# A hybrid decoder trunk on one core: 512- and 256-column matmuls in turns, and one set of PSUM pools

## The chip, the core and the metric

The kernel runs on one core of a Trainium2 chip. The metric is the device time of the whole program in microseconds (us), as the median of several runs. The engines are TensorE (PE, with its weight loads shown apart as PEld), VectorE (DVE), ScalarE (ACT), GpSimd (POOL) and SyncE (SP), whose queue issues the weight transfers here.

## The reference

256 tokens of width 2048 go through two layers in float32: layer 0 has a differential attention mixer, layer 1 a Mamba-2 mixer (SSM), and each is followed by a squared-ReLU MLP with a hidden width of 8192. Every sub-layer is preceded by an RMS norm and added to the residual.

```python
def rms_norm(x, gain):
    return x * lax.rsqrt(jnp.mean(x * x, axis=-1, keepdims=True) + EPS) * gain

def sq_relu_mlp(h, w1, w2):
    return jnp.square(jax.nn.relu(h @ w1)) @ w2
...
for i in range(DEPTH):
    x = x + mixer[i % 2](rms_norm(x, mixer_norm[i]))
    x = x + sq_relu_mlp(rms_norm(x, mlp_norm[i]), w1[i], w2[i])
```

Nearly all arithmetic lies in the products with weight matrices: the attention's q, k, v and output projections, the SSM's input and output projections, and the two matrices of each MLP.

## The kernel before, in words

**Precision.** A float32 weight tile of 128x1024 is fetched into `raw` (four buffers, by SP's queue) and split into a high part, an ACT copy (L158), and a low part, what is left, a DVE subtraction (L159); both halves lie in one tile `w` (four buffers). Activations are split in the same way, so that an activation tile holds 256 columns of high and 256 columns of low parts. A product is then high weight by both parts (512 columns) plus low weight by the high part (256 columns), summed in PSUM in float32.

**`sub_block` (L161 to L173)** multiplies eight 128x128 weight tiles into one PSUM bank: first eight 512-column matmuls with the high weights (L168), then eight 256-column matmuls with the low weights (L172). It is called 354 times, which makes 2832 matmuls of each kind. `wide_pair` and `wide_one` call it for two output blocks side by side or for one: `wide_pair` goes through the first half of the inner dimension for both blocks and then through the second half for both.

**`token_block` (L208 to L226)** is the other form, in which tokens are the stationary operand: 512 columns throughout (L222 and L224), two PSUM banks that fill side by side. It serves v, the output projections and the MLP's second matrix. `residual` (L293, and L610 in the MLP of layer 0) then adds the two banks into the tile `h` on DVE. Half of each MLP's first matrix goes through `seven` (L536 to L538), which forms seven products for a 2x2 block scheme in seven PSUM banks at once, 512 columns each; its operands are sums that DVE makes (L529 to L532 for weights, L492 to L503 for activations).

**Side work.** `Side` holds two queues of Python generators. Every `side.tick()` inside `sub_block` or `token_block` lets the first generator of each queue write down its next piece. That, and a scheduler in the compiler that may move ready matmuls ahead, sets the order of instructions on the engines. In `sub_block` the ticks stand after the fourth and the eighth 512-column matmul and after the eighth 256-column one. `norm_input` (L259) is such a generator: once a 512-column block of `h` is complete, it transposes it on PE (L268, four 128x128 transposes into an `aux` bank, twice), and `x_parts` makes the next stage's activations out of it (ACT, and DVE in L250). It gives back one tick before the first four transposes.

**PSUM.** It has eight banks. In the attention and SSM stages a pool gives four to matrix products (`mm`), another three to small work (`aux`) and one to `aux1`. Each MLP closes these and opens a pool of eight `mm` banks (the function `psum_pools`), and the SSM opens the former kind again. The first tile of a new pool waits for whatever was still using that bank in the old one.

Of the kernel before, what the change touches and what calls it, by code (L numbers as in the profile page):

```python
# [12 lines left out]
F32 = mybir.dt.float32  # L13
# [7 lines left out]
P = 128  # L21
# [67 lines left out]
def trunk_kernel(ctx: ExitStack, tc: tile.TileContext, x, xt, par, rope, qk, wv, wo, w10, w10s, w20, win, wdt, wout, w11, w11s, w21, out):  # L89
# [3 lines left out]
    const = ctx.enter_context(tc.tile_pool(name="const", bufs=1))  # L93
    actp = ctx.enter_context(tc.tile_pool(name="actp", bufs=1))
    wp = ctx.enter_context(tc.tile_pool(name="wp", bufs=1))
    psum = {}

    def psum_pools(stack, one):

        psum["mm"] = stack.enter_context(tc.tile_pool(name="ps_mm", bufs=8 if one else 4, space=PSUM))  # L100
        psum["ax"] = None if one else stack.enter_context(tc.tile_pool(name="ps_ax", bufs=3, space=PSUM))

    pa = const.tile([P, NPAR], F32, name="pa")
    nc.scalar.dma_start(out=pa[:, 0:C_MLP0], in_=par[:, 0:C_MLP0])
# [9 lines left out]
    G.affine_select(out=tri, in_=ones, pattern=[[1, P]], compare_op=ALU.is_ge, fill=0.0, base=0, channel_multiplier=-1)  # L114

    def aux():
        if psum["ax"] is None:
            return psum["mm"].tile([P, 512], F32, tag="mm", name="aux")
        return psum["ax"].tile([P, 512], F32, tag="aux", bufs=3, name="aux")

    def aux1():
        return psum["ax"].tile([P, 512], F32, tag="aux1", bufs=1, name="aux1")

    def rows(dst, cols, name):

# [23 lines left out]
    def cols(j):  # L149
        return slice(NB * j, NB * (j + 1))  # L150
# [11 lines left out]
    def sub_block(w, acts, k0, acc, start, stop):  # L162

        wh, wl = w
        for k in range(8):
            while len(acts) <= k0 + k:
                side.tick()
            PE.matmul(acc, lhsT=wh[:, k * P:(k + 1) * P], rhs=acts[k0 + k], start=(start and k == 0), stop=False)  # L168
            if k % 4 == 3:
                side.tick()  # L170
        for k in range(8):
            PE.matmul(acc[:, 0, :], lhsT=wl[:, k * P:(k + 1) * P], rhs=acts[k0 + k][:, 0, :], start=False, stop=(stop and k == 7))  # L172
        side.tick()  # L173

    def load(src, n=1):

# [4 lines left out]
        return raw  # L181

    def bank():
        return psum["mm"].tile([P, 2, T], F32, tag="mm", name="pp")

    def wide_pair(src, b, acts):

# [70 lines left out]

    def norm_input(j, gain, xs):  # L259

        for i in range(2):
            if i == 0:
                yield
            ax = aux().rearrange("p (a b) -> p a b", a=2)
            for f in range(2):
                for t in range(2):
                    c = NB * j + T * i + P * f
                    PE.transpose(ax[:, f, t * P:(t + 1) * P], h[:, t, c:c + P], ident)  # L268
            xs += x_parts(ax, 2 * j + i, gain)
            yield  # L270
        norm_square(j)
# [22 lines left out]

    scope = ExitStack()
    psum_pools(scope, False)
    xs = []
    first = [bank() for _ in range(2)]  # L300
    raw = []
# [180 lines left out]
            residual(token_block(rng(wo, 4, 8), j, sum((heads[i] for i in range(4, 8)), [])), j)  # L482
            side.add(norm_input(j, C_MLP0, xs))

    scope.close()


    def sum_parts(pool, x, dst):

# [68 lines left out]
    def mlp(xs, w1, w1s, w2, pool, after):  # L558
# [22 lines left out]
        for q in range(4):  # L581
            hid = []
            p7 = None
            wait_for = 2 if q == 0 else 0
            for j in range(8 + wait_for):
                if j >= wait_for:
                    i = j - wait_for
                    while len(sas) <= i:
                        side.tick()
                    if i == 0:  # L590
                        p7 = [bank().rearrange("p a b -> p (a b)") for _ in range(7)]
                    seven(pool, w1s[q, i], sas[i], p7, i == 0, i == 7)
                    if i == 7:
                        u = seven_out(pool, p7)
                if j < 8:
                    if j % 2 == 0:
                        r = pool.tile([P, 2, T], F32, tag="relu2", bufs=1, name="relu")
                    add_sums(r[:, j % 2:j % 2 + 1], [wide_one(w1, 8 * q + j, xs)])
                    if j % 2:
                        if q == 0 and j == 1:  # L600
                            norm_mean()
                            V.reciprocal(out=r2, in_=ms)
                        V.scalar_tensor_tensor(out=r, in0=r, scalar=0.0, in1=r, op0=ALU.max, op1=ALU.mult)
                        hid += split_pair(r)
            side.add(hidden(u, hid))
            for j in range(4):
                src = rng(w2, 8 * q + 4, 8 * q + 8) + rng(w2, 8 * q, 8 * q + 4)
                pp = token_block(src, j, hid)
                for t in range(2):
                    V.scalar_tensor_tensor(out=h[:, t, cols(j)], in0=pp[t], scalar=r2[:, t:t + 1], in1=h[:, t, cols(j)],  # L610
                                           op0=ALU.mult, op1=ALU.add)
                    if q == 3:
                        after(j, t)
# [5 lines left out]
            side.add(norm_input(j, C_MIX1, xs_next))  # L619

    with tc.tile_pool(name="mlp0", bufs=1) as mp:
        with ExitStack() as scope:
            psum_pools(scope, True)
            mlp(xs, w10, w10s, w20, mp, to_mixer)
    xs = xs_next


    scope = ExitStack()
    psum_pools(scope, False)
    with tc.tile_pool(name="ssm", bufs=1) as sp:  # L630
        dram_a = tc.dram_tile([64, T], F32, name="dram_a")
        rstd = sp.tile([P, T], F32, name="rstd")
# [237 lines left out]
        out_part(3, True)  # L870
    xs = xs_next

    scope.close()
    with tc.tile_pool(name="mlp1", bufs=1) as mp:
        with ExitStack() as scope:
            psum_pools(scope, True)
            mlp(xs, w11, w11s, w21, mp, lambda j, t: nc.sync.dma_start(out=out[:, t, cols(j)], in_=h[:, t, cols(j)]))

# [95 lines left out]
```

## Time and profile before

| what | value |
|---|---|
| median of 3 runs | 2483.77 us (2481.91 to 2486.58) |
| the profiled execution's own time | 2483.01 us |
| its span in the trace | 2481.3 us |
| granted TensorE clock, mean over the span | 1.000 |
| PE busy | 2456.4 us (99%) |
| DVE busy | 1967.4 us (79%) |
| ACT busy | 1411.4 us (57%) |
| DMA, mean rate | 190 GB/s |

The span is divided into stages by what PE does: attention up to about 412 us, the first MLP to about 1105, the SSM to about 1787, the second MLP to the end. In the rows further down, a timeline row gives start and duration of a run of like instructions; matmuls are pipelined, so that durations of neighbours overlap and the difference of two starts is what they took. In brackets stands the idle time before the instruction and what ended it. `128*128 128x512` means a stationary tile of 128x128 and 512 moving columns on 128 partitions.

### The profile page before, as it was taken

The page shows a single profiled execution, that of the slowest core. Times are in us where ns is not written, and L with a number is a line of the kernel's source. Part 1 is how long each engine was busy: PE and PEld are TensorE (multiplying, and loading weights), DVE is VectorE, ACT ScalarE, POOL GpSimd, SP SyncE. Part 2 cuts the span into 40 slices and gives each one's busy share as a digit, 9 for nine tenths or more (in the row PEclk, how much of TensorE's full clock was granted, in tenths as well). Part 3 has the DMA queues.
Part 4 walks back from the last instruction along what each step waited for, and adds up shares of the span by engine and source line. Part 5 has one row for each costly group of instructions (what it writes and reads, how often), then busy time and mean ns, then how long its engine had stood idle before and what let it go on. Part 6 is the DMA issues. An engine that isn't in the chain of part 4 may idle for free.

```text
span 2481.3 us, 33043 instructions
## 1 busy us (share of the span) xinstructions
PE 2456.4 (99%) x12462; PEld 2070.8 (83%) x12462; DVE 1967.4 (79%) x2558; ACT 1411.4 (57%) x2007; POOL 1.2 (0%) x8
## 2 busy tenths in 40 slices
PE   7999999999999999999999999999999999999999
PEld 6888887888888888888888888888788888888887
DVE  6788879977968949759886887887998696795874
ACT  6666656645545536556776576675565454554553
POOL 0000000000000000000000000000000000000000
PEclk9999999999999999999999999999999999999999
DMA  7445555465565555556555556455555556556554
GB/s 253 159 159 189 169 173 186 176 230 180 198 211 193 202 178 204 170 179 203 197 189 194 172 190 207 159 189 191 192 204 201 182 194 212 190 199 197 186 185 155
DMA packets 131120, 471.21 MB, mean 190 GB/s; under 512 B 14640, under 2 KB 14832, under 8 KB 130960
## 3 DMA queue, kind: packets, MB, share of 16 engines
q1 hardware_dynamic: 127152, 458.28, 54.8%
q10 hardware_dynamic: 3808, 10.81, 1.4%
q8 instruction: 98, 1.61, 0.3%
q14 instruction: 62, 0.51, 0.1%
HBM read 466.88 MB, written 2.16 MB: 189 GB/s over the span
## 4 chain that ended last, share of the span: by engine, by line
PE 96%; DVE 2%; DMA 1%; issue 0%; ACT 0%; ACTq 0%; SPq 0%; DVEq 0%
PE pp L222 27%; PE pp L168 26%; PE pp L172 14%; PE pp L224 13%; PE pp L536 4%; PE pp L537 4%; PE pp L538 4%; DVE w L159 1%; PE aux L774 1%; PE aux L576 1%; PE aux L141 0%; PE aux L408 0%; DMA raw<-in_w11s 0%; DMA h<-in_xt 0%; PE aux L268 0%
## 5 line engine op out<-in xcount | busy, mean ns | idle before, releaser
L159 DVE TENSOR_TENSOR w<-raw,w 128x1024 fp32r<-128x1024 f32 (+1 forms) x739 | 896.3, 1220 | 344.8 <-ACT w L158 341.8
L158 ACT CAST w<-raw 128x1024 fp32r<-128x1024 f32 (+1 forms) x739 | 776.2, 1051 | 594.9 <-PE pp L222 451.6
L222 PE MATMUL pp<-w,act 128*128 128x512 f32 x3072 | 962.7, 392 | 0.0
L168 PE MATMUL pp<-act,w 128*128 128x512 f32 x2832 | 721.7, 394 | 17.2 <-DVE act L250 13.0
L222 PEld LDWEIGHTS pp<-w,act 128*128 128x128 f32 x3072 | 574.7, 188 | 118.7 <-issue 2.1
L168 PEld LDWEIGHTS pp<-act,w 128*128 128x128 f32 x2832 | 511.5, 189 | 114.8 <-ACT w L158 17.9
L224 PE MATMUL pp<-w,act 128*128 128x512 f32 x1536 | 598.5, 390 | 0.0
L172 PEld LDWEIGHTS pp<-act,w 128*128 128x128 f32 x2832 | 384.7, 190 | 28.1 <-issue 1.7
L172 PE MATMUL pp<-act,w 128*128 128x256 f32 x2832 | 398.2, 283 | 0.0
L522 ACT CAST w<-raw 128x1024 fp32r<-128x1024 f32 (+1 forms) x256 | 241.3, 946 | 196.4 <-PE pp L172 111.0
L224 PEld LDWEIGHTS pp<-w,act 128*128 128x128 f32 x1536 | 288.6, 188 | 58.0
L523 DVE TENSOR_TENSOR w<-raw,w 128x1024 fp32r<-128x1024 f32 (+1 forms) x256 | 272.2, 1087 | 41.5 <-ACT w L522 38.5
L536 PE MATMUL pp<-w,sa 128*128 128x512 f32 x256 | 99.9, 390 | 0.0
L537 PE MATMUL pp<-w,sa 128*128 128x512 f32 x256 | 99.8, 390 | 0.0
L538 PE MATMUL pp<-w,sa 128*128 128x512 f32 x256 | 99.6, 389 | 0.0
L529 DVE TENSOR_TENSOR raw<-raw 128x1024 f32<-128x1024 f32 x64 | 78.1, 1221 | 6.8 <-DMA raw<-in_w10s 3.8
L537 PE MATMUL pp<-w,act 128*128 128x512 f32 x192 | 75.2, 391 | 0.0
L536 PE MATMUL pp<-w,act 128*128 128x512 f32 x192 | 75.1, 391 | 0.0
L538 PE MATMUL pp<-w,act 128*128 128x512 f32 x192 | 74.7, 389 | 0.0
L699 DVE SCALAR_TENSOR_TENSOR cy<-u,cwb,cy 128x256 f32<-128x256 f32 x144 | 62.9, 480 | 1.4
L205 ACT COPY relu<-pp 128x256 f32<-128x256 f32 x64 | 23.9, 373 | 63.9 <-PE pp L172 63.9
L536 PEld LDWEIGHTS pp<-w,sa 128*128 128x128 f32 x256 | 48.1, 188 | 10.5
(210 smaller groups left out, 1665.1 us busy)
## 6 DMA issues: line engine op xcount, KB each, us to landing
raw<-in_w SPq DMA_DIRECT2D x384, 512.0 KB, 3.9
raw<-in_win SPq DMA_DIRECT2D x160, 512.0 KB, 3.4
raw<-in_wout SPq DMA_DIRECT2D x64, 512.0 KB, 3.4
raw<-in_qk SPq DMA_DIRECT2D x63, 512.0 KB, 3.4
raw<-in_w10s SPq DMA_DIRECT2D x32, 768.0 KB, 4.4
raw<-in_w11s SPq DMA_DIRECT2D x32, 768.0 KB, 4.4
raw<-in_wv SPq DMA_DIRECT2D x32, 512.0 KB, 4.1
raw<-in_wo SPq DMA_DIRECT2D x32, 512.0 KB, 3.8
```

The source lines that it names most:

```text
L158: S.copy(out=wh[:, s], in_=raw[:, s])
L159: V.tensor_tensor(out=wl[:, s], in0=raw[:, s], in1=wh[:, s].bitcast(F32), op=ALU.subtract)
L168: PE.matmul(acc, lhsT=wh[:, k * P:(k + 1) * P], rhs=acts[k0 + k], start=(start and k == 0), stop=False)
L172: PE.matmul(acc[:, 0, :], lhsT=wl[:, k * P:(k + 1) * P], rhs=acts[k0 + k][:, 0, :], start=False, stop=(stop and k == 7))
L222: PE.matmul(pp[t], lhsT=act[:, 0, tok], rhs=m, start=(s + i + k == 0), stop=(s == n - 1 and i + k == 2))
L224: PE.matmul(pp[t], lhsT=act[:, 1, tok], rhs=m, start=False, stop=False)
L522: S.copy(out=w[:, 0], in_=r[:, a:a + n, :])
L523: V.tensor_tensor(out=w[:, 1], in0=r[:, a:a + n, :], in1=w[:, 0].bitcast(F32), op=ALU.subtract)
L529: V.tensor_tensor(out=r[:, 3:5, :], in0=r[:, 0:2, :], in1=bc(r[:, 6, :], 2), op=ALU.subtract)
L536: PE.matmul(pp[n], lhsT=ah, rhs=wh, start=start, stop=False)
L537: PE.matmul(pp[n], lhsT=al, rhs=wh, start=False, stop=False)
L538: PE.matmul(pp[n], lhsT=ah, rhs=wl, start=False, stop=stop)
```

## The change

Four edits:

1. In `sub_block` each step k issues its 512-column matmul and its 256-column matmul one behind the other. The three ticks stand after k = 2, 5 and 7.
2. One PSUM pool serves the whole kernel: four `mm`, three `aux` and one `aux1` bank. `psum_pools` and its scopes are gone. The seven banks of `seven` are three `mm`, three `aux` and the `aux1`.
3. `norm_input` gives back three ticks before its first transposes instead of one.
4. In each MLP the first two blocks of the first matrix that go through `wide_one` one after the other go through one `wide_pair`.

The number of instructions on each engine stays the same. The diff, without the parts that only remove the scopes:

```diff
-    psum = {}
-
-    def psum_pools(stack, one):
-
-        psum["mm"] = stack.enter_context(tc.tile_pool(name="ps_mm", bufs=8 if one else 4, space=PSUM))
-        psum["ax"] = None if one else stack.enter_context(tc.tile_pool(name="ps_ax", bufs=3, space=PSUM))
+    ps = ctx.enter_context(tc.tile_pool(name="ps", bufs=4, space=PSUM))
...
     def aux():
-        if psum["ax"] is None:
-            return psum["mm"].tile([P, 512], F32, tag="mm", name="aux")
-        return psum["ax"].tile([P, 512], F32, tag="aux", bufs=3, name="aux")
+        return ps.tile([P, 512], F32, tag="aux", bufs=3, name="aux")
...
         for k in range(8):
             while len(acts) <= k0 + k:
                 side.tick()
-            PE.matmul(acc, lhsT=wh[:, k * P:(k + 1) * P], rhs=acts[k0 + k], start=(start and k == 0), stop=False)
-            if k % 4 == 3:
+            kk = slice(k * P, (k + 1) * P)
+            PE.matmul(acc, lhsT=wh[:, kk], rhs=acts[k0 + k], start=(start and k == 0), stop=False)
+            PE.matmul(acc[:, 0, :], lhsT=wl[:, kk], rhs=acts[k0 + k][:, 0, :], start=False, stop=(stop and k == 7))
+            if k in (2, 5, 7):
                 side.tick()
-        for k in range(8):
-            PE.matmul(acc[:, 0, :], lhsT=wl[:, k * P:(k + 1) * P], rhs=acts[k0 + k][:, 0, :], start=False, stop=(stop and k == 7))
-        side.tick()
...
     def bank():
-        return psum["mm"].tile([P, 2, T], F32, tag="mm", name="pp")
+        return ps.tile([P, 2, T], F32, tag="mm", bufs=4, name="pp")
...
     def norm_input(j, gain, xs):
 
+        yield from wait(3)
         for i in range(2):
-            if i == 0:
-                yield
...
                     if i == 0:
-                        p7 = [bank().rearrange("p a b -> p (a b)") for _ in range(7)]
+                        p7 = [t for _ in range(3) for t in (bank().rearrange("p a b -> p (a b)"), aux())] + [aux1()]
...
-                    add_sums(r[:, j % 2:j % 2 + 1], [wide_one(w1, 8 * q + j, xs)])
+                    if q or j > 1:
+                        add_sums(r[:, j % 2:j % 2 + 1], [wide_one(w1, 8 * q + j, xs)])
+                    elif j == 0:
+                        add_sums(r, wide_pair(w1, 0, xs))
```

In the new file the lines move: L168 and L172 become L162 and L163, L222 and L224 become L214 and L216, L268 becomes L259, L141 becomes L134.

Three places show the order that results, all on PE. A row gives line, result, operands and shape; x2 or x4 are repetitions. First the end of the attention's output projection, where a block of `h` (`h_77`, or `h_80` after) is transposed while the next block (`pp_3517` and `pp_3518`, or `pp_3514` and `pp_3515`) is multiplied. Before:

```order
L222 MATMUL pp_3517<-w_3521,act_2371 128x512
L224 MATMUL pp_3517<-w_3521,act_2371 128x512
L222 MATMUL pp_3518<-w_3521,act_2371 128x512
L224 MATMUL pp_3518<-w_3521,act_2371 128x512
L268 MATMUL aux_3532<-ident_68,h_77 128x128 x4
L222 MATMUL pp_3517<-w_3521,act_2371 128x512
L222 MATMUL pp_3518<-w_3521,act_2371 128x512
...
L268 MATMUL aux_3546<-ident_68,h_77 128x128 x4
```

After:

```order
L214 MATMUL pp_3514<-w_3518,act_2368 128x512
L214 MATMUL pp_3515<-w_3518,act_2368 128x512
...
L214 MATMUL pp_3515<-w_3535,act_2705 128x512
L216 MATMUL pp_3515<-w_3535,act_2705 128x512
L259 MATMUL aux_3542<-ident_71,h_80 128x128 x4
L214 MATMUL pp_3514<-w_3535,act_2705 128x512
L216 MATMUL pp_3514<-w_3535,act_2705 128x512
...
L259 MATMUL aux_3556<-ident_71,h_80 128x128 x4
```

Between the block's first matmul and the first four transposes stood 8 matmuls of 512 columns, now 16.

Second, the opening of the first MLP: the last matmul of the output projection, and the first block of the MLP's first matrix. Before:

```order
L222 MATMUL pp_3614<-w_3692,act_3344 128x512
L168 MATMUL pp_3720<-act_3441,w_3725 128x512 x2
...
L168 MATMUL pp_3720<-act_3551,w_3725 128x512 x2
L268 MATMUL aux_3740<-ident_68,h_77 128x128 x4
L172 MATMUL pp_3720<-act_3441,w_3725 128x256 x2
...
L268 MATMUL aux_3762<-ident_68,h_77 128x128 x4
L168 MATMUL pp_3720<-act_3633,w_3775 128x512 x2
```

After:

```order
L214 MATMUL pp_3611<-w_3689,act_3341 128x512
L162 MATMUL pp_3712<-act_3451,w_3718 128x512
L163 MATMUL pp_3712<-act_3451,w_3718 128x256
...
L162 MATMUL pp_3713<-act_3451,w_3748 128x512
...
L163 MATMUL pp_3713<-act_3465,w_3748 128x256
L259 MATMUL aux_3757<-ident_71,h_80 128x128 x4
L162 MATMUL pp_3713<-act_3465,w_3748 128x512
...
L259 MATMUL aux_3777<-ident_71,h_80 128x128 x4
```

The last transposes stood behind eight matmuls of the first block; now a whole sub-block of the first (`pp_3712`) and three pairs of the second block (`pp_3713`) stand ahead of them.

Third, a place in the attention, the start of a sub-block of a new pair of heads. Before:

```order
L168 MATMUL pp_956<-act_180,w_1012 128x512 x2
...
L168 MATMUL pp_957<-act_180,w_1041 128x512 x2
L168 MATMUL pp_957<-act_188,w_1041 128x512
L172 MATMUL pp_956<-act_180,w_1012 128x256
L141 MATMUL aux1_1005<-sqr_975,ones_r_73 128x512
```

After:

```order
L162 MATMUL pp_953<-act_177,w_1009 128x512
L162 MATMUL pp_954<-act_177,w_1038 128x512
L214 MATMUL pp_1062<-w_1066,act_117 128x512
L216 MATMUL pp_1062<-w_1066,act_117 128x512
L397 MATMUL aux_1077<-qkn_577 128x128
...
L134 MATMUL aux1_1002<-sqr_976,ones_r_76 128x512
L163 MATMUL pp_953<-act_177,w_1009 128x256
L162 MATMUL pp_953<-act_177,w_1009 128x512
```

The first 256-column matmul of `w_1012` stood behind eleven 512-column ones; that of `w_1009` stands behind two of them and some matmuls of other work (`pp_1062` and `pp_1063` of a `token_block`, `aux_1077` of the attention scores).

## Rows read from the trace of the kernel before

**Rows 1.** The profile's page: busy time of each engine with its share of the span and instructions, and the line that divides the chain of work that ended last by engine.

```profile
PE 2456.4 (99%) x12462; PEld 2070.8 (83%) x12462; DVE 1967.4 (79%) x2558; ACT 1411.4 (57%) x2007; POOL 1.2 (0%) x8
...
PE 96%; DVE 2%; DMA 1%; issue 0%; ACT 0%; ACTq 0%; SPq 0%; DVEq 0%
```

**Rows 2.** PE's waits, grouped by what ended them: engine, result, line; waited for: us in total, times, longest us.

```profile
PE aux L268 <- DVE h L293: 3.3, 3, 1.9
PE pp L168 <- DVE h L293: 2.8, 2, 1.6
PE pp L168 <- DVE h L610: 1.4, 1, 1.4
```

**Rows 3.** The page's costliest groups: the 256-column matmuls of `sub_block`; count, busy us, mean ns of one, idle before.

```profile
L172 PE MATMUL pp<-act,w 128*128 128x256 f32 x2832 | 398.2, 283 | 0.0
```

**Rows 4.** PE's timeline from 1007 us, where a `sub_block` follows 512-column matmuls and a second one follows the first: start, duration, instruction, count.

```profile
1007.78 1.98 PE L168 MATMUL pp<-act,w 128*128 128x512 f32 x8
1009.59 1.12 PE L172 MATMUL pp<-act,w 128*128 128x256 f32 x8
1010.54 2.00 PE L168 MATMUL pp<-act,w 128*128 128x512 f32 x8
1012.38 1.11 PE L172 MATMUL pp<-act,w 128*128 128x256 f32 x8
1013.34 0.40 PE L222 MATMUL pp<-w,act 128*128 128x512 f32 x1
```

**Rows 5.** PE's timeline at two lone 256-column matmuls (L141) within 512-column ones, in the attention.

```profile
134.76 0.40 PE L141 MATMUL aux<-sor,ones_r 128*128 128x256 f32 x2
135.00 0.39 PE L222 MATMUL pp<-w,act 128*128 128x512 f32 x1
...
135.68 0.39 PE L224 MATMUL pp<-w,act 128*128 128x512 f32 x1
```

**Rows 6.** The same in the SSM.

```profile
1322.93 0.40 PE L141 MATMUL aux<-ysr,ones_r 128*128 128x256 f32 x2
1323.17 0.39 PE L222 MATMUL pp<-w,act 128*128 128x512 f32 x1
...
1324.09 1.30 PE L222 MATMUL pp<-w,act 128*128 128x512 f32 x5
```

**Rows 7.** PE's timeline in the first MLP, a lone 512-column matmul within 256-column ones.

```profile
422.48 0.40 PE L168 MATMUL pp<-act,w 128*128 128x512 f32 x1
422.71 1.46 PE L172 MATMUL pp<-act,w 128*128 128x256 f32 x11
424.01 0.63 PE L168 MATMUL pp<-act,w 128*128 128x512 f32 x2
```

**Rows 8.** PE's timeline in the first MLP: sixteen transposes in a row and the matmul behind them.

```profile
506.60 1.91 PE L576 MATMUL aux<-ident,u 128*128 128x128 f32 x16
508.26 0.48 PE L222 MATMUL pp<-w,act 128*128 128x512 f32 x1
```

**Rows 9.** The three openings of a stage with new PSUM pools on PE's timeline, at 412, 1105 and 1787 us, and DVE's timeline at the first.

```profile
411.92 1.07 PE L222 MATMUL pp<-w,act 128*128 128x512 f32 x4
414.57 2.09 PE L168 MATMUL pp<-act,w 128*128 128x512 f32 x8 [1.58 <-DVE h L293]
...
413.14 1.28 DVE L293 TENSOR_TENSOR h<-pp,h 128x512 f32<-128x512 f32 x2
...
1104.13 1.07 PE L222 MATMUL pp<-w,act 128*128 128x512 f32 x4
1106.57 2.08 PE L168 MATMUL pp<-act,w 128*128 128x512 f32 x8 [1.37 <-DVE h L610]
...
1786.73 1.07 PE L222 MATMUL pp<-w,act 128*128 128x512 f32 x4
1789.04 1.16 PE L168 MATMUL pp<-act,w 128*128 128x512 f32 x4 [1.25 <-DVE h L293]
```

**Rows 10.** PE's timeline at the second norm transposes of the attention, and DVE's there.

```profile
388.04 0.39 PE L224 MATMUL pp<-w,act 128*128 128x512 f32 x1
390.35 0.33 PE L268 MATMUL aux<-ident,h 128*128 128x128 f32 x1 [1.93 <-DVE h L293]
390.95 0.55 PE L268 MATMUL aux<-ident,h 128*128 128x128 f32 x3 [0.27 <-DVE h L293]
...
381.90 1.23 DVE L529 TENSOR_TENSOR raw<-raw 128x1024 f32<-128x1024 f32 x1 [2.94 <-DMA raw<-in_w10s]
...
389.61 1.28 DVE L293 TENSOR_TENSOR h<-pp,h 128x512 f32<-128x512 f32 x2
```

**Rows 11.** The same place in the SSM: PE, then DVE.

```profile
1752.19 0.39 PE L224 MATMUL pp<-w,act 128*128 128x512 f32 x1
1753.69 0.33 PE L268 MATMUL aux<-ident,h 128*128 128x128 f32 x1 [1.11 <-DVE h L293]
...
1751.81 1.23 DVE L529 TENSOR_TENSOR raw<-raw 128x1024 f32<-128x1024 f32 x1 [1.36 <-DMA raw<-in_w11s]
```

**Rows 12.** The attention at 105 us: PE's timeline, and DVE's split of the weights that PE multiplies there.

```profile
105.50 2.68 PE L168 MATMUL pp<-act,w 128*128 128x512 f32 x11
108.02 0.32 PE L172 MATMUL pp<-act,w 128*128 128x256 f32 x1
...
106.69 2.34 DVE L159 TENSOR_TENSOR w<-raw,w 128x1024 fp32r<-128x1024 f32 x2
```

More of the change, by code (lines that the diff above doesn't have):

```diff
@@ L116, in aux @@
     def aux():
-        if psum["ax"] is None:
-            return psum["mm"].tile([P, 512], F32, tag="mm", name="aux")
-        return psum["ax"].tile([P, 512], F32, tag="aux", bufs=3, name="aux")
+        return ps.tile([P, 512], F32, tag="aux", bufs=3, name="aux")
     def aux1():
-        return psum["ax"].tile([P, 512], F32, tag="aux1", bufs=1, name="aux1")
+        return ps.tile([P, 512], F32, tag="aux1", bufs=1, name="aux1")
     def rows(dst, cols, name):
@@ L293, in residual @@
             V.tensor_tensor(out=h[:, t, cols(j)], in0=pp[t], in1=h[:, t, cols(j)], op=ALU.add)
-    scope = ExitStack()
-    psum_pools(scope, False)
     xs = []
@@ L483, in trunk_kernel @@
             side.add(norm_input(j, C_MLP0, xs))
-    scope.close()
     def sum_parts(pool, x, dst):
@@ L621, in trunk_kernel @@
     with tc.tile_pool(name="mlp0", bufs=1) as mp:
-        with ExitStack() as scope:
-            psum_pools(scope, True)
-            mlp(xs, w10, w10s, w20, mp, to_mixer)
+        mlp(xs, w10, w10s, w20, mp, to_mixer)
     xs = xs_next
-    scope = ExitStack()
-    psum_pools(scope, False)
     with tc.tile_pool(name="ssm", bufs=1) as sp:
@@ L871, in trunk_kernel @@
     xs = xs_next
-    scope.close()
     with tc.tile_pool(name="mlp1", bufs=1) as mp:
-        with ExitStack() as scope:
-            psum_pools(scope, True)
-            mlp(xs, w11, w11s, w21, mp, lambda j, t: nc.sync.dma_start(out=out[:, t, cols(j)], in_=h[:, t, cols(j)]))
+        mlp(xs, w11, w11s, w21, mp, lambda j, t: nc.sync.dma_start(out=out[:, t, cols(j)], in_=h[:, t, cols(j)]))
 def _units(b):
```

## The prediction

> **What bounds the kernel now.** I read the page's busy times first, then the chain that ended last, then PE's waits, and only then single places on the timelines. PE is busy for 99% of the span and makes up 96% of the chain; DVE has 2% of it [rows 1]. So an edit counts only if it shortens the rows of matmuls themselves or one of the few stretches in which PE stands. The granted clock is 1.000 over the whole span, so the clock has nothing to give back. Besides the start of the kernel, PE's waits that end in DVE's residual are 3.3 + 2.8 + 1.4 us [rows 2]. That is all the idle time within reach, and the rest of the answer lies in the spacing of 2832 pairs of matmuls.
>
> For spacing I take differences of starts, not durations: the 283 ns of a 256-column matmul [rows 3] overlap its neighbours. In a `sub_block`, eight 512-column matmuls behind other 512-column ones take 1009.59 - 1007.78 = 1.81 us, which is 0.227 each; the eight of 256 columns take 0.95, or 0.119 each; the next eight of 512 columns take 1.84, because they come behind 256-column ones, and their eight of 256 columns take 1013.34 - 1012.38 = 0.96 [rows 4].
>
> **Alternation, the term with the largest stake.** It removes no matmul. What it can win is the cost of going from one kind to the other: 1.84 against 1.81, of which 0.01 comes back in the 256-column run, leaves 0.02 us per `sub_block`. For 354 of them that is 354 x 0.02 = 7.1 us. What it may cost is that the kernel now goes back and forth eight times per `sub_block`. The trace of before has no such row of turns, so I bound it by short mixes. Two lone 256-column matmuls in the attention take 0.24 us, and the next three of 512 columns take 135.68 - 135.00 = 0.68, which is 3 x 0.227: no cost [rows 5]. The same in the SSM takes 0.24, but the next four of 512 columns take 1324.09 - 1323.17 = 0.92 against 0.907: 13 ns [rows 6]. A lone 512-column matmul among 256-column ones takes 0.23, and the eleven behind it 1.30 against 11 x 0.12 = 1.32: no cost, or 20 ns gained [rows 7]. So a return costs between 0 and 13 ns, two rows out of three say 0, and the row of eight says that a return costs more the longer the 256-column run before it was. I take 0: alternation gives 7.1 us. If the cost goes with the number of 256-column matmuls, however they are placed (0.02 / 8 = 2.5 ns each), it gives nothing. At the upper bound it takes 2832 x 0.013 = 36.8 us and gives back the 7.1.
>
> There is a price that no row isolates, the load of the stationary tile. The 256-column matmul has 0.119 us in which to hide the next load, and sixteen 128-column transposes in a row need 508.26 - 506.60 = 1.66 us, 0.104 each, although each loads a tile too [rows 8]. So loading a tile can take no more than 0.104. The Trainium skill, page "TensorE: Matmul & The Clock Gate", section "LDWEIGHTS (loading the stationary operand)", puts a load at columns / 1.2 ns, which is an estimate of 107 ns for 128 columns, close to the spacing in this row. By that rule runs of 256 columns would stand near the limit of loading, and a 512-column matmul between them would give the loads room; what that would bring is the third rival below. Against it the row shows that 512 columns, with more than twice the time for a load, carry the same overhead over columns at 2.4 GHz (227 - 213 = 14 ns) as 256 columns do (120 - 107 = 13 ns) [rows 4].
>
> **The cover that alternation takes away.** The low half of a weight tile, which DVE makes last, was needed eight 512-column matmuls after the high half; now it is needed 0.23 us after. Where DVE is late, that shows. At 105.50 us PE begins a tile whose low half is finished only at 106.69 + 1.17 = 107.86 (two splits in 2.34), against 105.50 + 0.23 = 105.73: 2.1 us late [rows 12]. The place comes three times in the attention, once per 76 us. In the order of after, matmuls of a `token_block` and of the scores stand in that gap, so the scheduler has found other work. I put it at 0, with an upper bound of 3 x 2.1 = 6.4 us. Elsewhere weights are split well ahead and four `w` buffers stay as they are.
>
> **One set of PSUM pools.** At three openings the first matmul waits until the residual has read the last banks of the old pool. Four 512-column matmuls take 0.907, so PE could go on at 412.83 and goes on at 414.57: 1.74 us. In the same way 1106.57 - 1105.04 = 1.53 and 1789.04 - 1787.64 = 1.40 [rows 9]. Together 4.67 us. With a common pool of four `mm` banks the next block takes the two banks that the last `token_block` doesn't use, so the wait goes. What is late next is the activations: the last block of `h` must still be added, transposed and split before its two activation tiles are needed. In the order of after, a whole sub-block and three pairs, (8 + 3) x 0.347 = 3.8 us, stand ahead of the last transposes, whereas DVE is through with the residual by 413.14 + 1.28 = 414.42 [rows 9], 1.6 us after PE's last `token_block` matmul. That covers the MLPs. The SSM opens with `wide_one`, with less in front: I allow 0.35 us there and up to 0.5 at each MLP. This is also what the fourth edit, the pair at the start of the MLP, is worth: its second block's first half covers the transposes. By itself it is put at 0; without it the transposes would need the activations some 2.8 us earlier and the 4.67 us would come back in part.
>
> `seven` held seven of eight banks before and holds seven now; the eighth is `mm` in both. The small work of the stages has three `aux` banks as in the mixers before. Put at 0, at most a few tenths.
>
> **Norm transposes later.** At 388 us PE should go on at 388.04 + 0.23 = 388.27 and starts the transpose at 390.35; between the first and the three others another 0.60 - 0.11 = 0.49 is lost: 2.57 us. DVE had stood for 2.94 us behind a subtraction that waits for a weight transfer, and the residual got its turn at 389.61 only [rows 10]. At 1752 us the same happens: 1753.69 - 1752.42 = 1.27 [rows 11]. Together 3.84. Two more ticks let eight more 512-column matmuls go ahead, 8 x 0.227 = 1.81 us, and in the order of after the residual has less ahead of it on DVE. Eight matmuls don't quite cover 2.08 us, but with the shorter queue I expect the whole 3.84 to go. What queues behind the transposes is `x_parts` and with it the next activations, 1.8 us later; only the last block of a stage feels that, and it is counted above.
>
> **Sum.** Edges: -4.67 - 3.84 + 1.5 (0.35 + 2 x 0.5, and 0.15 for what is left of the transposes' wait) = -7.0. Alternation: -7.1. Together -14.1, so 2483.0 - 14.1 = 2468.9 for an execution like the profiled one. That execution is 0.8 below the median of the three runs, so on the median's scale it is **2470**.
>
> **The rivals.**
> First, alternation changes nothing, since the cost goes with the number of 256-column matmuls: 2470 + 7 = 2477, still faster, by the edges alone. For it: the excess behind a run is small, and 13 ns behind only two [rows 6] is more than two eighths of it. Against: rows 5 and 7 show none.
> Second, slower: each return to 512 columns costs what it does in the SSM, 13 ns. 2470 + 36.8 = 2507; at half of that price 2470 + 18.4 = 2488. It decides from 14.1 / 2832 = 5.0 ns per pair, that is from a pair of 0.347 + 0.0025 = 0.350 us, since from there on the win at the edges is eaten. It needs no event, only a price that one row of three shows.
> Third, 256-column runs were held up by loads: with 512-column matmuls between them each would fall from 0.119 to the transposes' 0.104 at the lowest [rows 8], so up to 2832 x 0.015 = 42 us: 2470 - 42 = 2428. Against it: the equal overheads of both widths.
> Fourth, low halves arrive too late in the attention: 2470 + 6.4 = 2476. For it: 2.1 us of lateness [rows 12]; against: other matmuls stand there in the order.
> Fifth, the change doesn't do what it says at the norm: DVE is held by the same weight transfer and the transposes wait as before: 2470 + 3.8 = 2474.
>
> **How the numbers follow.** My forecast 2470 has 0.46, the first rival 0.20, the second 0.15, the third 0.05, the fourth 0.08, the fifth 0.06. A measurement of this kernel can tell about 0.2%, 5 us, from no change: faster is below 2478.8, slower above 2488.7. Faster: 0.46 + 0.05 + 0.06, and of the first and fourth, which lie 2 us from the edge, 0.15: 0.72. Slower: most of the second rival, 0.12, and 0.02 for the first and fourth falling together with new waits: 0.14. The rest, 0.14, is within. The range must leave out 2 in 10: the third rival below (0.05), and the second at its full price above (0.13). So it goes from 2470 - 11 = 2459 (no new waits, and alternation that also gains as in rows 7, some 3 ns per pair) to 2488 (the second at half its price).
>
> **What would show it.** In the profile of the changed kernel a pair of 512 and 256 columns takes 0.347 us where nothing waits; 0.350 or more proves the second rival, 0.331 the third. PE's waits for `h` at the openings are gone or under 0.5 each. No idle time of 1 us stands before the norm transposes. In the attention, near the three places, a wait of PE for the low half (DVE's split) would prove the fourth. The prediction is wrong if pairs are not uniform, for instance if the spacing depends on the stage, or if idle time appears at the openings that the last activations cause.

## The result, and the profile after

| | before | after |
|---|---|---|
| median of 21 runs each | 2481.71 us (2479.57 to 2486.58) | 2485.88 us (2484.58 to 2487.81) |
| ratio | | 1.0017, 95% interval 1.0011 to 1.0023 |
| span of the profiled execution | 2481.3 us | 2482.9 us |

The changed kernel is 4 us slower, 0.17%, which is less than the 0.2% that the prediction calls no change. It was forecast at 2470 us and faster; the time lies inside the range, on the other side of no change. The page of the profile after, busy times first, then the chain that ended last:

```profile
PE 2465.9 (99%) x12462; PEld 2070.2 (83%) x12462; DVE 1967.3 (79%) x2558; ACT 1410.0 (57%) x2007; POOL 1.2 (0%) x8
...
PE 99%; DMA 1%; DVE 0%; ACT 0%; issue 0%; SPq 0%; DVEq 0%
```

PE's busy time grew by 9.5 us with the same 12462 instructions, and DVE's share of the chain went from 2% [rows 1] to 0. So idle time left PE, and more than that came back inside its matmuls. The view of PE's waits agrees (engine, result, line, releaser; us in total, times, longest):

```profile
PE pp L162 <- DVE act L242: 12.3, 1, 12.3
PE pp L163 <- DVE w L152: 0.3, 1, 0.3
```

Only the start of the kernel and 0.3 us behind it are left; the waits for `h` [rows 2] are gone. The two places look as the prediction wanted them. PE's timeline at the second norm transposes (start, duration), and DVE's residual there:

```profile
390.72 0.39 PE L216 MATMUL pp<-w,act 128*128 128x512 f32 x1
390.95 0.60 PE L259 MATMUL aux<-ident,h 128*128 128x128 f32 x4
...
388.13 1.28 DVE L284 TENSOR_TENSOR h<-pp,h 128x512 f32<-128x512 f32 x2
```

The transposes follow the matmul before them after 0.23 us, where 2.3 had passed [rows 10]; the residual is through at 389.41, 1.5 us ahead of them.

What came back is in the pairs. PE's timeline in the SSM, three turns of one `sub_block`:

```profile
1382.84 0.40 PE L162 MATMUL pp<-act,w 128*128 128x512 f32 x1
1383.07 0.28 PE L163 MATMUL pp<-act,w 128*128 128x256 f32 x1
1383.19 0.40 PE L162 MATMUL pp<-act,w 128*128 128x512 f32 x1
1383.43 0.28 PE L163 MATMUL pp<-act,w 128*128 128x256 f32 x1
1383.55 0.40 PE L162 MATMUL pp<-act,w 128*128 128x512 f32 x1
1383.79 0.28 PE L163 MATMUL pp<-act,w 128*128 128x256 f32 x1
1383.90 0.40 PE L162 MATMUL pp<-act,w 128*128 128x512 f32 x1
```

From the first 512-column start to the last are 1.06 us for three pairs, 0.353 each. To the nanosecond the three are 350, 361 and 349, and this sequence of three repeats without a break through 139 pairs from 1343 us on, almost 50 us. Yet the same instructions also run at the sum of their parts. The same timeline at the beginning of the SSM:

```profile
1131.11 0.39 PE L162 MATMUL pp<-act,w 128*128 128x512 f32 x1
1131.34 0.27 PE L163 MATMUL pp<-act,w 128*128 128x256 f32 x1
1131.45 0.40 PE L162 MATMUL pp<-act,w 128*128 128x512 f32 x1
1131.68 0.28 PE L163 MATMUL pp<-act,w 128*128 128x256 f32 x1
1131.80 0.39 PE L162 MATMUL pp<-act,w 128*128 128x512 f32 x1
```

Two pairs take 0.69 us, 0.345 each by these rounded rows; in nanoseconds they are 343 and 350 in turn, 346.7 on average, held for 78 pairs from 1114 to 1141 us. So a pair has two speeds, 346.7 and 353.3 ns, and most pairs run at the second.

Added up over the whole trace, as differences of PE's starts, the matmuls of `sub_block` take 999.9 us before and 1010.3 after, and everything else on PE 1464.2 and 1455.5: +10.4 and -8.7, with the first matmul 0.2 us earlier, makes the +1.6 of the spans. The medians differ by 4.2, since the profiled execution of after is the fastest of its 21 and that of before lies 1.3 us above its median; so these sums tell where the time goes, and the medians how much it is. A warning on the groups: they can't be used for this. Those of after say (count, busy us, mean ns of one, idle before)

```profile
L162 PE MATMUL pp<-act,w 128*128 128x512 f32 x2832 | 1013.7, 401 | 12.3 <-DVE act L242 12.3
L163 PE MATMUL pp<-act,w 128*128 128x256 f32 x2832 | 794.9, 281 | 0.3 <-DVE w L152 0.3
```

794.9 us against the 398.2 of before [rows 3], with 281 ns for one instead of 283: a group's busy time merges overlapping neighbours of its own group, and in turns no neighbour is of the same group.

### The profile page after: what moved, and what is told of

The parts are those of the page before. It is cut to its first block, busy times and chain, and to the rows that moved or that the text cites. A ratio compares the mean times of both kernels' runs of the same rounds, so it can differ in the third digit from the quotient of the medians.

```text
span 2482.9 us, 33046 instructions
## 1 busy us (share of the span) xinstructions
PE 2465.9 (99%) x12462; PEld 2070.2 (83%) x12462; DVE 1967.3 (79%) x2558; ACT 1410.0 (57%) x2007; POOL 1.2 (0%) x8
## 4 chain that ended last, share of the span: by engine, by line
PE 99%; DMA 1%; DVE 0%; ACT 0%; issue 0%; SPq 0%; DVEq 0%
PE pp L214 28%; PE pp L162 27%; PE pp L216 14%; PE pp L163 13%; PE aux L523 2%; PE aux L524 2%; PE aux L525 2%; PE pp L524 2%; PE pp L525 2%; PE pp L523 2%; PE aux L760 1%; PE aux L563 1%; PE aux L397 0%; PE aux L134 0%; PE aux L259 0%; DMA raw<-in_qk 0%
## 5 line engine op out<-in xcount | busy, mean ns | idle before, releaser
L152 DVE TENSOR_TENSOR w<-raw,w 128x1024 fp32r<-128x1024 f32 (+1 forms) x739 | 895.3, 1219 | 342.3 <-ACT w L151 339.7
L162 PE MATMUL pp<-act,w 128*128 128x512 f32 x2832 | 1013.7, 401 | 12.3 <-DVE act L242 12.3
L214 PE MATMUL pp<-w,act 128*128 128x512 f32 x3072 | 960.8, 392 | 0.0
L163 PE MATMUL pp<-act,w 128*128 128x256 f32 x2832 | 794.9, 281 | 0.3 <-DVE w L152 0.3
L214 PEld LDWEIGHTS pp<-w,act 128*128 128x128 f32 x3072 | 574.5, 188 | 119.1 <-issue 2.1
L162 PEld LDWEIGHTS pp<-act,w 128*128 128x128 f32 x2832 | 532.8, 188 | 143.3 <-ACT w L151 12.3
L216 PE MATMUL pp<-w,act 128*128 128x512 f32 x1536 | 598.6, 390 | 0.0
L163 PEld LDWEIGHTS pp<-act,w 128*128 128x128 f32 x2832 | 535.8, 189 | 5.9 <-DVE w L152 2.4
L216 PEld LDWEIGHTS pp<-w,act 128*128 128x128 f32 x1536 | 288.5, 188 | 57.9
L523 PE MATMUL aux<-w,sa 128*128 128x512 f32 x192 | 75.0, 391 | 0.0
L524 PE MATMUL aux<-w,sa 128*128 128x512 f32 x192 | 74.9, 390 | 0.0
L525 PE MATMUL aux<-w,sa 128*128 128x512 f32 x192 | 74.7, 389 | 0.0
L600 DVE SCALAR_TENSOR_TENSOR h<-pp,r,h 128x512 f32<-128x512 f32 x64 | 45.1, 746 | 12.9 <-PE pp L214 12.9
L524 PE MATMUL pp<-w,act 128*128 128x512 f32 x128 | 50.2, 393 | 0.0
L523 PE MATMUL pp<-w,act 128*128 128x512 f32 x128 | 50.1, 392 | 0.0
L525 PE MATMUL pp<-w,act 128*128 128x512 f32 x128 | 49.8, 389 | 0.0
```

What stands on the lines that cost most here:

```text
L152: V.tensor_tensor(out=wl[:, s], in0=raw[:, s], in1=wh[:, s].bitcast(F32), op=ALU.subtract)
L162: PE.matmul(acc, lhsT=wh[:, kk], rhs=acts[k0 + k], start=(start and k == 0), stop=False)
L163: PE.matmul(acc[:, 0, :], lhsT=wl[:, kk], rhs=acts[k0 + k][:, 0, :], start=False, stop=(stop and k == 7))
L214: PE.matmul(pp[t], lhsT=act[:, 0, tok], rhs=m, start=(s + i + k == 0), stop=(s == n - 1 and i + k == 2))
L216: PE.matmul(pp[t], lhsT=act[:, 1, tok], rhs=m, start=False, stop=False)
L523: PE.matmul(pp[n], lhsT=ah, rhs=wh, start=start, stop=False)
```

## The experiments

Theory A: the turns cost 10 us, the edges give back 8 to 9, and the two add. Rival B: the dearer pairs come from the common pool. Then a second question: is the price one of the turn itself (fixed per return to 512 columns, or per lone 256-column matmul), of other engines' memory traffic, or of how a stretch of turns is entered?

**e1, the edges alone.** In the changed kernel:

```diff
-            PE.matmul(acc, lhsT=wh[:, kk], ...)
-            PE.matmul(acc[:, 0, :], lhsT=wl[:, kk], ...)
-            if k in (2, 5, 7):
+            PE.matmul(acc, lhsT=wh[:, k * P:(k + 1) * P], ...)
+            if k % 4 == 3:
                 side.tick()
+        for k in range(8):
+            PE.matmul(acc[:, 0, :], lhsT=wl[:, k * P:(k + 1) * P], ...)
+        side.tick()
```

Here and below, `...` stands for code that is left out.

> The changed kernel with the sub_block of before (eight 512-column matmuls, then eight of 256), so the edges alone: one set of PSUM pools, later norm transposes, the first two MLP blocks side by side. Theory A: a pair in turns costs 0.353 us in most stretches against 0.349 before (+10 us in all), and the edges give back about 8. Then this kernel takes 2481.7 - 8 = 2474 (ratio 0.997), and PE has no wait for h left. Rival B: the dearer pairs come with the common PSUM pool, not with the turns; then this kernel's eight pairs take over 2.80 us and it is not faster than before (ratio 1.000 to 1.004).

Measured 2475.07 us, ratio 0.9969 (0.9957 to 0.9981), and no wait for `h`. A holds, B falls. Its timeline at the same place is that of the kernel before:

```profile
1381.00 2.00 PE L161 MATMUL pp<-act,w 128*128 128x512 f32 x8
1382.84 1.12 PE L165 MATMUL pp<-act,w 128*128 128x256 f32 x8
1383.79 2.00 PE L161 MATMUL pp<-act,w 128*128 128x512 f32 x8
```

1383.79 - 1381.00 = 2.79 us for eight pairs.

**e2, the turns alone.** The changed `sub_block` in the kernel before.

> The kernel before with the turns of 512 and 256 columns alone; pools, norm transposes and MLP opening stay as they were. Theory A: +10 us from the pairs, edges as before: 2481.7 + 10 = 2492 (ratio 1.004), most pairs at 0.353. Rival B: pairs at 0.347 here, ratio 0.997 to 1.000.

Measured 2493.60 us, ratio 1.0041 (1.0028 to 1.0053): 11.7 us slower. With e1's 6.9 us faster the two add to +4.8; the whole change measured +4.2. In e2's trace the `sub_block` matmuls take 1009.9 us, 10.0 more than before. PE's waits at the edges stand as before:

```profile
PE aux L267 <- DVE h L292: 3.0, 3, 1.7
PE pp L169 <- DVE h L292: 2.8, 2, 1.6
PE pp L169 <- DVE h L609: 1.4, 1, 1.4
```

**e3, turns of two; e4, single turns with the low matmul one step later; e5, turns of four.** All in the changed kernel; the orders of a `sub_block` are

```
e3  H0 H1 L0 L1  H2 H3 L2 L3  ...
e4  H0 H1 L0 H2 L1 H3 L2  ...  H7 L6 L7
e5  H0 H1 H2 H3 L0 L1 L2 L3  H4 ... H7 L4 ... L7
```

with H for 512 and L for 256 columns.

> The changed kernel with turns of two (512, 512, 256, 256) in sub_block. If the price of 6.6 ns belongs to each return from 256 to 512 columns, four of them per sub_block cost 26 ns against 20 before and 53 with single turns: 354 x 0.006 = +2 us on the edges alone, 2476 (ratio 0.998). If the price belongs to each 256-column matmul that stands near 512-column ones, it costs as much as the single turns: 2485 (ratio 1.0015). If it depends on how a stretch is entered, anything between no price (2467, ratio 0.994) and the full one.

> The changed kernel with the 256-column matmul of step k issued behind the 512-column one of step k+1 (512, 512, 256, 512, 256, ..., 512, 256, 256). Seven of eight 256-column matmuls still stand alone. With a fixed price per return: 8 x 6.6 ns per sub_block as before the shift, 2485 (ratio 1.0015). If the price depends on how a stretch of turns is entered (in the changed kernel a stretch entered behind two 256-column matmuls ran at 0.347 for 78 pairs, stretches entered from 512-column runs at 0.353): pairs at 0.347 and 2468 to 2474 (ratio 0.995 to 0.997).

> The changed kernel with turns of four (four 512-column matmuls, four of 256, twice per sub_block). Clean sub_blocks so far: 2.793 us with turns of eight, 2.787 with turns of two, mostly 2.830 with single turns. If the price goes with returns once two or more 256-column matmuls stand together, two returns cost less than four: 2.78 per sub_block, 2472 (ratio 0.996). If a return costs the more the longer the 256-column run before it was (20 ns behind eight, 3 behind two): about 10 ns twice, 2.793, as the edges alone: 2475 (0.997).

Measured: e3 2473.95 us, ratio 0.9965 (0.9952 to 0.9977); e4 2482.89, 1.0002 (0.9993 to 1.0011); e5 2479.78, 0.9990 (0.9981 to 0.9999). The timeline of e3 in the SSM:

```profile
1380.02 0.63 PE L162 MATMUL pp<-act,w 128*128 128x512 f32 x2
1380.49 0.39 PE L164 MATMUL pp<-act,w 128*128 128x256 f32 x2
1380.71 0.62 PE L162 MATMUL pp<-act,w 128*128 128x512 f32 x2
1381.18 0.40 PE L164 MATMUL pp<-act,w 128*128 128x256 f32 x2
1381.41 0.63 PE L162 MATMUL pp<-act,w 128*128 128x512 f32 x2
```

The same timeline of e5:

```profile
1380.98 1.09 PE L162 MATMUL pp<-act,w 128*128 128x512 f32 x4
1381.90 0.64 PE L166 MATMUL pp<-act,w 128*128 128x256 f32 x4
1382.38 1.09 PE L162 MATMUL pp<-act,w 128*128 128x512 f32 x4
1383.31 0.63 PE L166 MATMUL pp<-act,w 128*128 128x256 f32 x4
1383.78 1.09 PE L162 MATMUL pp<-act,w 128*128 128x512 f32 x4
```

Four pairs take 1.39 us in e3 and 1.40 in e5. From the starts in nanoseconds an uninterrupted `sub_block` takes, against 8 x (226.7 + 120) = 2774 without any loss:

| order | most frequent time of a sub_block, ns | over 2774, per return |
|---|---|---|
| eights (before, e1) | 2793 | 20 for one |
| fours (e5) | 2806 | 16 for each of two |
| twos (e3) | 2787 | 3 for each of four |
| ones (after, e2) | 2830 | 7 for each of eight |
| ones, the other speed | 2773 | 0 |

A return has no fixed price. Behind two, four and eight 256-column matmuls it grows, but not in proportion, so that fours are dearer in all than twos and eights; and single turns, at 7, don't fit into that order. e4 came out between its two expectations, nearer to the fixed price; its blocks take 2818 ns.

**e9 and e10, entry of a stretch of turns.** Changed kernel with one turn of two per `sub_block`: at its end (e9: H6 H7 L6 L7) or at its beginning (e10: H0 H1 L0 L1), single turns for the other six steps.

> The changed kernel with single turns for k = 0 to 5 and one turn of two for k = 6 and 7 at the end of each sub_block, so that each stretch of single turns is entered behind two 256-column matmuls of the same bank kind. If the price of 6.6 ns is fixed for a return from a lone 256-column matmul: six of them and one of 3.3 ns, 43 ns per sub_block, 2.817 us, 2475 + 354 x 0.024 = 2483.5 (ratio 1.0005). If it is set by how a stretch is entered: the single turns run at 0.347, sub_blocks take 2.775 to 2.785, 2469 to 2473 (ratio 0.995 to 0.9965).

> The same with the turn of two at the beginning of each sub_block (k = 0 and 1) and single turns for k = 2 to 7. Fixed price: 2.817 us per sub_block, 2483.5 (ratio 1.0005). Set by the entry: 2.775 to 2.785, 2469 to 2473 (ratio 0.995 to 0.9965); the two kernels need not agree, since the first matmul of a bank comes at another point of the turn.

Measured: e9 2481.24, ratio 0.9998 (0.9989 to 1.0007), nearer to the fixed price; e10 2477.89, 0.9982 (0.9974 to 0.9991), between the two expectations. The stretch of 78 pairs that suggested these two kernels has four 128-column matmuls directly ahead of it, with two 256-column ones further back, so they don't repeat its entry. e10's blocks show why it came out in between. In the SSM from 1116 us on they take, one behind the other, 2817, 2776, 2817, 2777, 2816, 2777 ns, and in the first MLP 2807 and 2777 in turn, the same sixteen matmuls each time. Its timeline in a cheap one:

```profile
1130.44 0.63 PE L161 MATMUL pp<-act,w 128*128 128x512 f32 x2
1130.91 0.28 PE L163 MATMUL pp<-act,w 128*128 128x256 f32 x1
1131.03 0.27 PE L165 MATMUL pp<-act,w 128*128 128x256 f32 x1
1131.14 0.40 PE L161 MATMUL pp<-act,w 128*128 128x512 f32 x1
...
1131.49 0.39 PE L161 MATMUL pp<-act,w 128*128 128x512 f32 x1
...
1132.88 0.39 PE L161 MATMUL pp<-act,w 128*128 128x512 f32 x1
```

Five single turns from 1131.14 to 1132.88 take 0.348 each. Equal sequences thus have two times in strict alternation. In the SSM the dear and the cheap blocks go to the two PSUM banks of a pair in turn, but in the first MLP they are the two halves of one `wide_one`, which share a bank; so the bank doesn't decide. What fits is that a block is entered in one of two states and leaves the other to the next. No run sets such a state directly.

**e11, without the weight traffic.** In the changed kernel:

```diff
-            raw = [load(src[b + t, s]) for t in range(2)]
...
-                sub_block(split_weights(raw[t]), acts, ...)
+                sub_block((still[:, 0, :], still[:, 1, :]), acts, ...)
```

The same is done in `wide_one`, and the `w` tiles that are left have three buffers instead of four.

> The changed kernel with one weight tile, written once, used by every wide_pair and wide_one: the weight transfers, the ACT copies and the DVE subtractions of those sub_blocks are left out, so the products are those of other weights. It asks whether the dear turns come from other engines' and the transfers' use of memory. If so, the pairs fall to 0.347 us, 354 x 0.045 = 16 us less than the changed kernel in the sub_blocks. If the dear turns are TensorE's own, the same three pairs of 0.361, 0.349 and 0.350 stand in most of the stretches, and only waits change.

One run: 2484.13 us, and the same three pairs at the same place (350, 361, 349 ns; start to start by these rows 0.35, 0.35, 0.36):

```profile
1382.82 0.40 PE L162 MATMUL pp<-act,still 128*128 128x512 f32 x1
...
1383.17 0.40 PE L162 MATMUL pp<-act,still 128*128 128x512 f32 x1
...
1383.52 0.40 PE L162 MATMUL pp<-act,still 128*128 128x512 f32 x1
...
1383.88 0.40 PE L162 MATMUL pp<-act,still 128*128 128x512 f32 x1
```

The `sub_block` matmuls take 1010.2 us in all, as in the changed kernel (1010.3), although between 1343 and 1392 us the transfers move 30 GB/s instead of 197. The stretch of 78 pairs at 346.7 ns is there too. So the weight transfers and splits of these blocks have no part in the price, and neither has the place of the weight tile, since there is only one.

**e6, e7, e8, the edges one by one.** All with turns of eight. e6: `norm_input` with `wait(1)`, `wide_one` at the MLP's start; e7: `wait(3)`, `wide_one`; e8: `wait(1)`, `wide_pair`.

> The kernel before with the common PSUM pool alone: turns of eight, one tick ahead of the norm transposes, the first MLP blocks one after the other. By the prediction's steps the three waits at the openings (4.67 us) go, but without the second block's cover part of them comes back, and the transposes' wait (3.84) stays: 2481.9 - 4.7 + 1 to 3 = 2478 to 2480 (ratio 0.9985 to 0.9995). Rival: the openings' waits are all that the edges give, and the other two edits nothing: 2474 to 2475 (0.997).

> Common pool and three ticks ahead of the norm transposes, turns of eight, first MLP blocks one after the other. By the prediction's steps: the transposes' 3.84 us go, while at the MLP openings the transposes and the activations come late without the second block's cover, 0.5 to 2.8 us each: 2475 to 2480 (ratio 0.997 to 0.999). Rival: the side-by-side blocks are worth nothing, 2475 (0.997).

> Common pool and the first MLP blocks side by side, turns of eight, one tick ahead of the norm transposes. By the prediction's steps the transposes wait as before: 2475 + 3.8 = 2478.9 (ratio 0.9985). Rival: the common pool alone brings the residual forward on DVE, and the later ticks are worth nothing: 2475 (0.997).

Measured: e6 2476.76, ratio 0.9980 (0.9971 to 0.9989); e7 2476.12, 0.9974 (0.9964 to 0.9984); e8 2477.84, 0.9984 (0.9976 to 0.9993). Outside of `sub_block`, PE's time is 1464.2 us before, 1457.6 in e6, 1456.4 in e7, 1461.2 in e8 and 1455.8 in e1. These are sums of one trace each; by the medians the 95% intervals of e6, e7 and e8 overlap, so the small differences among them are what the traces show and no more. The pool gives 6.6 of e1's 8.4. The later transposes give 1.2 on top of it, since with the pool alone the first of the two places has shrunk and the second is gone from PE's waits; e6's row:

```profile
PE aux L260 <- DVE h L285: 1.4, 2, 1.1
```

In e8's trace the same place is worse than before. PE's timeline:

```profile
388.25 0.39 PE L217 MATMUL pp<-w,act 128*128 128x512 f32 x1
391.18 1.50 PE L260 MATMUL aux<-ident,h 128*128 128x128 f32 x4 [2.54 <-DVE h L285]
392.33 2.05 PE L215 MATMUL pp<-w,act 128*128 128x512 f32 x4
394.19 0.77 PE L260 MATMUL aux<-ident,h 128*128 128x128 f32 x4
```

And the view by stretches, with the busy time and count of PE, PEld, DVE, ACT and POOL, the granted clock, the DMA share and GB/s:

```profile
391.00:393.00 2.00, 1.70 (x6) 1.31 (x7) 2.00 (x5) 1.73 (x5) 0.00 (x0) 0.53 0.73 262
```

The transposes start 391.18 - 388.25 = 2.93 us after the matmul before them, 0.6 us later than in the kernel before [rows 10], because DVE reaches the residual later. Then the granted clock is 0.53 over two microseconds, and the four 512-column matmuls take 394.19 - 392.33 = 1.86 us, where the same four take 1.02 in the kernel before.

It would be wrong to put the lower clock down to the longer wait. e2's trace has it at the same place, after a shorter one (two rows of PE's timeline, and the view by stretches):

```profile
389.35 0.39 PE L223 MATMUL pp<-w,act 128*128 128x512 f32 x1
391.41 0.33 PE L267 MATMUL aux<-ident,h 128*128 128x128 f32 x1 [1.67 <-DVE h L292]
...
393.00:396.00 3.00, 3.00 (x11) 2.42 (x10) 3.00 (x7) 2.69 (x5) 0.00 (x0) 0.50 0.58 201
```

There PE stood for 391.41 - 389.35 = 2.06 us from start to start, less than the 2.31 of the kernel before, whose clock stayed at 1.00.

In the traces e8 is slower than e6 by 3.5 us outside of `sub_block`. Of these 1.8 are longer waits for `h` (3.2 against 1.4) and about 1.3 the lower clock, which not every execution has: in three of e8's eleven runs, the profiled one among them, the mean granted clock of the span is 0.999, in the others 1.000. By the medians e8 is 1.1 us slower than e6. So it isn't shown that the side-by-side blocks and the later transposes depend on each other; with the later transposes, e1's trace is ahead of e7's by 0.6. Why DVE's work at 388 us should move with the MLP's blocks, 23 us behind it, was not tested; e8's trace shows that DVE again waits for a weight transfer there, 3.55 us before L517.

**e12, longer runs.** e1's kernel, with `wide_pair` issuing the high matmuls of both blocks (16) and then the low ones (16).

> The edges of the change, and in wide_pair the sixteen 512-column matmuls of both blocks followed by their sixteen of 256 columns; wide_one as before. A return behind sixteen 256-column matmuls costs 20 ns as one behind eight does, so half of the returns in the paired sub_blocks go: about 135 pairs x 0.02 = 2.7 us below the edges alone, 2472 (ratio 0.996), unless the low halves come too late or the price grows with the run, then 2475 (0.997).

Measured 2476.18 us, ratio 0.9978 (0.9969 to 0.9987), not better than e1. An uninterrupted double block does take 5567 ns instead of 2 x 2793, as expected, but the `sub_block` matmuls in all take 1001.5 us against 1000.1 in e1. PE has 1.6 us of new waits in it, 1.2 of them for low halves (L179 for DVE's L152, five times); the rest of what is missing from the expected 2.7 us has no cause shown.

The fastest version is e3, turns of two with the edges: 2473.95 us, 0.35% below the kernel before, and not told apart from e1.

## Why the prediction was wrong

**The step that failed** is "I take 0: alternation gives 7.1 us". A return from a lone 256-column matmul measured about 0 in stretches that hold some one pair in eight, and about 6.6 ns in the others. That lies within the bounds of 0 and 13 ns; the choice of 0 was wrong. The alternation term was -7.1 us and measured +10.4 (in the sums of starts; 10.0 in e2's) or +11.7 (e2's median). This is the second rival at about half of its price: it was given 2488, and 2485.88 came out. That the half fits is luck, since no row gave it.

I counted rows, two for 0 and one for 13, where the two lone 256-column matmuls of the attention [rows 5] and of the SSM [rows 6] are the same instruction, each within 512-column ones. That they differ was the finding. To the nanosecond the trace of before shows it more clearly than the rows as I read them: the next 512-column matmuls take 227, 227, 226 and 227 in the attention, but 226, 236, 228, 232 and 231 in the SSM, which is 20 ns lost and not 13, since I stopped one matmul early. And each place repeats its price. At all five places of the attention where such a pair stands behind a run of 512 columns it is free, at all eight of the SSM it is not. So the price hangs on something that the row doesn't show, and the value had to stay open between the signs.

The second rival's threshold was worked out wrongly in the prediction: 5.0 ns on top of 0.347 is a pair of 0.352 us, while 0.350 is where alternation alone wins nothing. Most pairs take 0.353, above both, so the sign that it named still told the right rival.

The picture behind the choice, that "a return costs more the longer the 256-column run before it was", holds for e3, e5 and the kernel before, with 3, 16 and 20 ns behind two, four and eight. It breaks where I used it: behind one it is 0 or 7.

**One set of pools**: 4.67 us were to go, and e6 gives 6.6 outside of `sub_block`. What more it gives lies at the transposes: with the pool alone their wait shrinks from 3.3 us [rows 2] to 1.4. I had put that to the ticks, whose 3.84 us were over-sized: on top of the pool they give 1.2 (e6 against e7). The new waits were over-sized: 0.35 at the SSM's opening and up to 0.5 at each MLP were allowed, and the trace of after has only one, at the SSM's opening: 0.465 us from the start of a 512-column matmul to the next, 0.24 more than a normal one.

**Later transposes**: all 3.84 us gone, as forecast, but about half of that by the pool. "By itself it is put at 0" for the side-by-side blocks holds nearly: 0.6 us in the traces (e7 against e1). That without them the activations would be needed some 2.8 us earlier, and the 4.67 us come back in part, doesn't show: e6 and e7 have no wait for `h` at the openings.

**The edges in all**: -7.0 forecast, -8.7 in the trace, -6.9 in the medians of e1. The waits went as described and the size holds; the shares of pool and ticks do not.

**The other rivals.** Low halves too late in the attention: PE's waits after show 0.3 us for them, at the start of the kernel and not at the three places, where the scheduler put other work, as the order said. Loads at their limit: no pair came below 0.340, so 0.331 is excluded. The row behind it was misread, too: to the nanosecond the transposes of [rows 8] stand 108 to 110 apart, and only the last is followed after 28 by the next matmul, so that 0.104 is a mean of unequal spacings. The rule of the Trainium skill, page "TensorE: Matmul & The Clock Gate", section "LDWEIGHTS (loading the stationary operand)", columns / 1.2 ns, gives no ground for either speed of a pair: with an estimate of 107 ns, both loads of a pair fit into 347 ns; no run here isolates a load. Transposes that wait as before: excluded.

**What stays open** is what sets the speed of a pair. Shown is that it isn't the common pool (e2 has the same pairs), not weight transfers and splits (e11), and not the sequence of matmuls in a block (e10, one block after the other at 2777 and 2807 or 2817). Nor is it the activation tiles: the 78 fast pairs and the 139 slow ones both belong to the SSM's input projection and go through the same sixteen. A stretch keeps its speed until other work or a delay interrupts it. With single turns, each of the 67 stretches behind twelve or more 512-column matmuls was slow; each of the seven behind only two of them was fast. A state that TensorE carries along would explain this, but that is an argument. For the two kinds of places in the trace of before [rows 5, rows 6], the tiles that they read and write differ as well, and no run separates the two.

## What to carry to other kernels

Where two nearest rows of the same instruction disagree, the price hangs on something that neither shows: look at every like place, to the last row in which the excess shows; multiply the whole spread by the count (here 2832), and if that changes the sign, say so in the chances. A reordering that only changes how matmuls of different widths follow one another is cheap to try and could not be argued here: turns of 1, 2, 4 and 8 gave 2486, 2474, 2480 and 2475 us. Separate a change into its parts before judging it: here 7 us of gain in the edges stood under 12 us of loss from the turns.

## What had not been expected of the hardware

Equal sequences of matmuls without any wait run at two speeds (346.7 and 353.3 ns for 512 and 256 columns, at full granted clock), in cycles of two and of three pairs that last for tens of microseconds.

At the attention's second norm transposes PE stood for 2.93 us from one matmul's start to the next in e8, for 2.06 in e2 and for 2.31 in the kernel before [rows 10]. In e8 and e2 the granted clock then fell to the lower level of 1.2 GHz, with 512-column matmuls 0.43 us apart; in the kernel before it stayed at 1.00. So the length of the stretch alone doesn't tell whether the clock falls, and no run here shows what does. Where it fell, it cost more than the wait: from the first transpose to the start of the second matmul behind the last one are 3.85 us in e8 and 2.59 in the kernel before, for the same instructions.
